# Forty instead of thirty-two tokens by gathered rows, the rest by dense products, in a transformer block with product-key experts

## The chip, the cores and the metric

One Trainium2 chip, one core of it. The metric is device time in microseconds (us) of one execution, lower is better; times given are medians of several runs.

## The reference

One block over 256 tokens of width 2048: latent attention and forgetting attention (8 heads each), a layer norm, and then the part that the change touches, a product-key expert layer ("peer") beside a gated embedding, and a last layer norm.

```python
def peer(h, w_q, keys1, keys2, u_tab, v_tab):          # h: 256 tokens x 2048
    q = (h @ w_q).reshape(b, s, 8, 128)
    s1, s2 = q[..., :64] . keys1, q[..., 64:] . keys2   # 128 scores each, per head
    v1, i1 = top_k(s1, 16); v2, i2 = top_k(s2, 16)
    sc, pos = top_k(all 256 sums of v1 and v2, 16)
    eidx = (i1 * 128 + i2) at pos                       # 16 experts of 16384, for each of 8 heads
    gate = softmax(sc)
    a   = sum_d u_tab[eidx] * h                         # 128 experts a token
    act = gelu(a) * gate
    return sum_k act * v_tab[eidx]                      # rows of 2048
h = layer_norm(ALPHA * h + peer(...) + (p @ w_proj) * sigmoid(h @ w_gate))
```

All of it is float32.

## The kernel before

The 16384 experts are 128 blocks of 128. For most tokens the kernel computes the products with **all** experts (dense) and multiplies by a gate matrix that is zero where an expert wasn't chosen. For the last `TS` = 32 tokens it gathers the rows that were chosen (sparse). `TD` = 256 - `TS` = 224 tokens are dense.

**The dense products.** A float32 weight tile of 128 x 2048 (1024 KB) is loaded by the SP queue into one of three raw buffers (line 74), and each half of it is split into a rounded part `hi` by ScalarE (line 79) and a remainder `lo` by VectorE (line 80), into five buffers of each. `Queue` hands out the halves in the order of use and makes three of them ahead. TensorE multiplies `hi` by the tokens' own hi and lo parts and `lo` by their hi part. For the first 24 u blocks these are three matmuls of `TD` columns for each 128 x 128 piece (`uprod`, line 715). After them come 104 u blocks (`uslots`) and 128 v blocks (`vslots`) in turn, as u, v, u, v, with 27 v blocks alone at the end. Here one matmul takes `hi` with both parts side by side, 2 x `TD` columns (lines 985 and 1015), and one takes `lo` with `TD` columns (lines 986 and 1016): sixteen such pairs for each block. A u block is summed (ScalarE line 974, VectorE line 975), goes through the Gelu (976), is multiplied by its gates (line 964) and split again (968, 969); a v block is added to the accumulator `accT` (998, 999). A u block is made three blocks ahead of its use.

**The gate matrix.** While the first 24 u blocks run, the one-hot products of eight tokens at a time (`gate_onehots`, then `gate_products`, line 769, `TB` = 8) build the gates, ScalarE moves them out of PSUM into `gsb` (line 774), and a group of `TG` = 32 tokens is stored to DRAM in two DMAs by SP (line 777). There are 28 such blocks and seven groups. In the dense products ScalarE's queue loads the gates of four u blocks in one DMA (`gload`, line 955; before the first u block it loads the first). Its destination is in a pool that takes the memory of the pool with the index and gate tiles `xe` and `gg`.

**The sparse tokens.** Each of the 32 tokens has 128 rows of `u` and of `v`. It lies on four partitions (`NQ` = 128 / `TS`), each with 32 of its rows (`NR_`). Lines 905 to 907 issue from POOL (GpSimd) the twelve DMAs that lay out the row numbers, the gates and the token's vector so. Then 64 steps follow, 32 for `u` and 32 for `v`: POOL gathers a row for each partition (line 935, three buffers), and VectorE takes the dot product with the token (line 942) or adds the row times its weight (949). A step stands in some v blocks, by

```python
if not half and ns < 2 * NR_ and (i + 1) * 2 * NR_ >= ns * (NK - NU - PRE - 2):
    sparse(ns)
    ns += 1
```

with `NK` - `NU` - `PRE` - 2 = 99, so that they are spread over the first 98 v blocks, and each step issues the gather three steps ahead. At the end a matmul with the constant `sel` adds the four partitions of each token (`add_y`, line 1048), `finish_columns` transposes the dense results back, and `norm2` does the last layer norm.

The instructions of each engine are issued in the order of the program in this part of the kernel (a manual order); each engine runs its own in order.

Of the kernel before, what the change touches and what calls it, by code (L numbers as in the profile page):

```python
# [16 lines left out]
AF = mybir.ActivationFunctionType  # L17
OP = mybir.AluOpType
AX = mybir.AxisListType

P = 128
# [21 lines left out]
CK = CC["swap"][0]  # L43


TS = 32
TD = T - TS
NQ = P // TS
CB = 8


@with_exitstack
def block_kernel(ctx: ExitStack, tc: tile.TileContext, xT, xn, cst, pos, wz, wkf, wfv, wuq, wuk, wuv, wo, wq, wg, wp,
                 pT, keysT, lnrows, ut, vt, un, vn, out):
    nc = tc.nc
    V, S, G, PE = nc.vector, nc.scalar, nc.gpsimd, nc.tensor
# [8 lines left out]
    def bank(tag, name):  # L65
        return (psA if tag == "A" else psum).tile([P, 512], F32, name=name, tag=tag,
                                                  bufs={"A": 4, "B": 2, "C": 2}[tag])
# [20 lines left out]
    def b8(name, shape, dt=F32):  # L88
        return keep.tile(shape, dt, name=name, tag="b8", bufs=4)
# [4 lines left out]
    def cc(name, p0=0, p1=P):  # L94
        a, b = CC[name]
        return cs[p0:p1, a:b] if b <= CK else cs1[p0:p1, a - CK:b - CK]
# [84 lines left out]
    for g in range(4):  # L181
# [6 lines left out]
        for k0 in range(4 * g, 4 * g + 4, step):  # L188
            c = slice(k0 % 8 * T, (k0 % 8 + step) * T)
            ks = slice(k0, k0 + step)  # L190
            r = xr[g // 2][:, c]
# [167 lines left out]
    for h in range(NH):  # L359
        q_, k_ = head_tile("fq"), head_tile("fk")  # L360
        zs = itertools.chain(zsteps(wz[8 + 2 * h], q_, xhl), zsteps(wz[9 + 2 * h], k_, xhl))
        for i in range(4):
# [7 lines left out]
            h, q_, k_, lambda qb, n, h=h: (fsel[0:F1, h:h + 1].to_broadcast([F1, P]), negF[0:F1, :n]),  # L370
# [50 lines left out]
    for hg in range(2):  # L421
# [4 lines left out]
        for j in range(4):  # L426
            h = hg * 4 + j
            r0 = 64 * (h % 2)
            for _ in attend(
                h, qn[j], kn[j],  # L430
                lambda qb, n, h=h, r0=r0: (qr[h // 2][r0:r0 + 64, qb * P:(qb + 1) * P], kr[r0:r0 + 64, :n]),
# [31 lines left out]
            self.used += 1  # L463
            return self.ready[self.used - 1]

    TG = 32
    TB = 8
    NU, PRE = 24, 3

    NC = NK // CB  # L470
    order = [("u", b) for b in range(NU, NU + PRE)]
# [21 lines left out]
    def tk(name, shape, dt=F32):  # L493
        return pg.tile(shape, dt, name=name, tag="tk", bufs=4)
# [32 lines left out]
    for i in range(2):  # L527
        for c in range(0, D, T):
            nc.sync.dma_start(lnr[i][:, c:c + T], bass.AP(tensor=lnrows.tensor, offset=lnrows.offset + i * D + c,
                                                          ap=[[0, P], [1, T]]))  # L530
# [113 lines left out]
    gst, sel = {}, {}  # L644
# [88 lines left out]

    ND = TD // TG
    gd = dram.tile([ND, P, NK, TG], F32, name="gd")
    iot = pg.tile([P, P, 2], F16, name="iot")
# [21 lines left out]
    def gate_products(b):  # L758
        o = onehot.pop(b)
        g, q = divmod(b, TG // TB)  # L760
        if q == 0:
            gsbs[g] = [b8("gsb", [P, NK // 2, TG]) for _ in range(2)]
        gsb = gsbs[g]
        for q4 in range(TB // 4):
# [7 lines left out]
            for i in range(2):  # L772
                t0 = q * TB + q4 * 4
                S.mul(gsb[i][:, :, t0:t0 + 4], gv[:, i * 64:(i + 1) * 64], 1.0 / GSCALE)
        if q == TG // TB - 1:
            for i in range(2):
# [34 lines left out]

    hd = dram.tile([TS, D], F32, name="hd")
    G.dma_start(hd, acc[P - TS:, 1])

# [39 lines left out]
    n = 0  # L854
# [35 lines left out]
            _, _, f_, a_ = later.pop(0)  # L890
            f_(*a_)

    NR_ = P // NQ
    xg = [tk("xg", [P, P]), tk("xe", [P, P], U32)]
    gi1, gg1 = gst[1][3], gst[1][4]
    V.scalar_tensor_tensor(xg[0], gi1[:, 0], float(NK), gi1[:, 1], op0=OP.mult, op1=OP.add)
    V.tensor_copy(xg[1], xg[0])
    xidx = p2.tile([P, NR_], U32, name="xidx")
    xgate = p2.tile([P, NR_], F32, name="xgate")
    dots = p2.tile([P, NR_], F32, name="dots")  # L900
    hy = b8("hy", [P, D])
    rows = [b8("rows", [P, D]) for _ in range(3)]
    for q in range(NQ):
        qs_, qc = slice(q * TS, (q + 1) * TS), slice(q * NR_, (q + 1) * NR_)
        G.dma_start(xidx[qs_], xg[1][P - TS:, qc])
        G.dma_start(xgate[qs_], gg1[P - TS:, qc])
        G.dma_start(hy[qs_], hd)

    ad = dram.tile([2, P, D], F32, name="ad")
# [15 lines left out]
    def defer(n, f_, *a_):  # L925
        slots[n].append((f_, a_))

    def slot():
        for f_, a_ in slots.pop(0):
            f_(*a_)  # L930
        slots.append([])

    def gather(i):
        if i < 2 * NR_:
            G.indirect_dma_start(out=rows[i % 3], out_offset=None, in_=(un if i < NR_ else vn),  # L935
                                 in_offset=bass.IndirectOffsetOnAxis(ap=xidx[:, i % NR_:i % NR_ + 1], axis=0))

    def sparse(i):

        r, j = rows[i % 3], slice(i % NR_, i % NR_ + 1)  # L940
        if i < NR_:
            V.scalar_tensor_tensor(r, r, 1.0, hy, op0=OP.mult, op1=OP.mult, accum_out=dots[:, j])  # L942
            if i == NR_ - 1:
                S.activation(dots, dots, AF.Gelu)
        elif i == NR_:
            V.tensor_tensor(dots, dots, xgate, op=OP.mult)
            V.tensor_scalar(hy, r, dots[:, j], None, op0=OP.mult)
        else:
            V.scalar_tensor_tensor(hy, r, dots[:, j], hy, op0=OP.mult, op1=OP.add)  # L949
        gather(i + 3)  # L950

    def gload(c):
        if c < NK // GC:
            gbs[c] = p3.tile([P, ND, GC, TG], F32, name="gb", bufs=2)
            nc.scalar.dma_start(gbs[c], bass.AP(tensor=gd.tensor, offset=gd.offset + c * GC * TG,
                                                ap=[[NK * TG, P], [P * NK * TG, ND], [1, GC * TG]]))

    def gated(b):
        c, j = divmod(b, CB)
        if b % GC == 0:  # L960
            gload(b // GC + 1)
        ga = gel.pop(b)
        gv = ga.rearrange("p (g t) -> p g t", t=TG)
        V.tensor_tensor(gv, gv, gbs[b // GC][:, :, b % GC], op=OP.mult)  # L964
        if j == 0:
            acts[c] = p3.tile([P, CB, 2, TD], F32R, name="act", bufs=2)
        at = acts[c][:, j]
        S.copy(at[:, 0], ga)  # L968
        defer(0, lambda: V.tensor_tensor(at[:, 1], ga, at[:, 0].bitcast(F32), op=OP.subtract))  # L969
# [33 lines left out]
    def vslots(i):  # L1003
# [4 lines left out]
        for g in range(2):  # L1008
            hi, lo = queue.get()
            for d in range(2):  # L1010
                o = ps[:, d, :2 * TD].rearrange("p (w t) -> p w t", w=2)
                for j4 in range(4):
                    j = g * 4 + j4
                    col = slice(j4 * 256 + d * P, j4 * 256 + (d + 1) * P)
                    PE.matmul(o, hi[:, col], at[:, j], start=j == 0, stop=False)  # L1015
                    PE.matmul(ps[:, d, :TD], lo[:, col], at[:, j, 0], start=False, stop=j == CB - 1)  # L1016
            slot()
# [27 lines left out]
    def add_y(q):  # L1045
        fin, qs_ = fins[0], slice(q * 512, (q + 1) * 512)
        ps = bank("C", "yps")
        PE.matmul(ps, cc("sel"), hy[:, qs_], start=True, stop=True)
        defer(0, lambda: V.tensor_tensor(fin[:, 1, qs_], fin[:, 1, qs_], ps, op=OP.add))


# [42 lines left out]
    for i in range(3):  # L1094
        gather(i)
    gload(0)
    ns, since = 0, 0
    for n, (w, i) in enumerate(order):
        for half, _ in enumerate(uslots(i) if w == "u" else vslots(i)):
            if n and n < PRE:  # L1100

                for b in range(2):
                    gated(((n - 1) * 2 + half) * 2 + b)
            elif w == "v":
                if half and i + CB < NK:
                    gated(i + CB)
# [4 lines that stand above are left out]
                if i >= NK - NU - PRE + 3 and not half:  # L1111
                    since += 1
                    if since == 1:
                        get_fin()
                    elif 5 <= since < 9:
                        add_y(since - 5)
# [6 lines left out]
def _constants():  # L1123
    c = np.zeros((P, CW), np.float32)
    i = np.arange(P)

    def put(name, a):
        c[:, CC[name][0]:CC[name][1]] = a

    put("ident", np.eye(P))  # L1130
    sw = (i // 64) * 64 + (i % 64 + 32) % 64
    perm = np.zeros((P, P))
    perm[sw, i] = 1.0
    put("swap", perm)
    dup = np.zeros((P, P))
    dup[i % 64, i] = 1.0
    put("dup", dup)
    dsw = np.zeros((P, P))
    dsw[(i % 64 + 32) % 64, i] = 1.0
    put("dupswap", dsw)  # L1140
    put("mean", np.full((P, P), 1.0 / 512))
    put("iota", np.tile(i[None, :], (P, 1)))
    put("sel", (i[None, :] >= P - TS) & (i[:, None] % TS == i[None, :] - (P - TS)))
    fsel = np.zeros((P, NH))
    for r in (0, 32, 64):
        fsel[r + np.arange(NH), np.arange(NH)] = 1.0
    put("fsel", fsel)
    put("mask", np.where(i[None, :] <= i[:, None], 0.0, NEG))
    e = np.arange(0, 64, 2, dtype=np.float32) / np.float32(64)
    freq = (np.float32(1) / np.power(10000.0, e.astype(np.float64)).astype(np.float32)).astype(np.float32)  # L1150
    put("freq", freq[i % 32][:, None])
    put("sign", np.where(i % 64 < 32, -1.0, 1.0)[:, None])
    return c


def _layout(x, p, positions, w_in, b_forget, g_q_norm, w_uq, g_kv_norm, w_ukv, w_out, ln1_g, ln1_b, peer_wq,
# [17 lines left out]
    d["xT"] = A(xt.transpose(1, 0, 2))  # L1174
    d["xn"] = A(x.reshape(2, P, D).transpose(1, 0, 2))
    cst = _constants()

    def put(name, a):
# [59 lines left out]
```

## Time and profile before

| | |
|---|---|
| median of 3 runs | 1937.49 us (1937.35 to 1937.9) |
| the profiled execution | 1937.41 us |
| its span, first to last instruction | 1935.6 us |
| mean granted TensorE clock | 0.983 |
| TensorE, VectorE, ScalarE, GpSimd busy | 96%, 77%, 48%, 15% of the span |
| DMA | 469.86 MB, 243 GB/s over the span |

PE is TensorE's matmuls and PEld its weight loads, DVE is VectorE, ACT is ScalarE, POOL is GpSimd, SP is the engine that issues most loads. A DMA's issue is listed with its queue (SPq, ACTq, or POOL). [...] Matmuls overlap, so the time of one is read from the distance of two starts. Idle time of an engine that doesn't set the pace costs nothing.

### The profile page before, as it was taken

What the parts mean: (1) busy time and instruction counts of PE and PEld (TensorE: products, weight loads), DVE (VectorE), ACT (ScalarE), POOL (GpSimd) and SP (SyncE); (2) the same over time, 40 slices, a digit from 0 to 9 for tenths busy, and PEclk for the clock granted to TensorE, in tenths of its full rate; (3) what the DMA queues carried; (4) which work ended last, traced back from release to release, by engine and by line L of the source; (5) the groups of instructions that cost most, each with busy time, mean ns of one, the idle gap of its engine ahead of it and who ended that gap; (6) DMA issues with size and microseconds to landing.
All of it is one profiled execution on the core that took longest, in us unless ns stands there. A gap on an engine that the chain in (4) does not pass through costs nothing.

```text
span 1935.6 us, 29855 instructions
## 1 busy us (share of the span) xinstructions
PE 1865.9 (96%) x11729; PEld 1708.4 (88%) x11729; DVE 1489.9 (77%) x2307; ACT 927.3 (48%) x1430; POOL 287.2 (15%) x179
## 2 busy tenths in 40 slices
PE   9999999989899997999999999999999999999995
PEld 6888877878699996999999999999999999999895
DVE  6365655689999946887888888788888888877777
ACT  5454544454355534454444454544454554554341
POOL 0343000388300011101110110011010111000001
PEclk9999999999899998999999999999999999999997
DMA  7544434545456788878888888888888888867651
GB/s 288 216 174 148 157 134 144 190 159 178 149 194 237 271 297 306 293 280 293 294 285 298 285 286 294 280 293 290 302 284 286 283 296 289 287 216 278 228 184 66
DMA packets 96925, 469.86 MB, mean 243 GB/s; under 512 B 8304, under 2 KB 39792, under 8 KB 43120
## 3 DMA queue, kind: packets, MB, share of 16 engines
q1 hardware_dynamic: 57168, 380.49, 54.4%
q0 software_dynamic: 9712, 68.46, 10.3%
q10 hardware_dynamic: 29904, 19.01, 3.2%
q8 instruction: 92, 1.51, 0.3%
q14 instruction: 49, 0.40, 0.1%
HBM read 448.75 MB, written 19.14 MB: 242 GB/s over the span
## 4 chain that ended last, share of the span: by engine, by line
PE 87%; DVE 8%; ACT 2%; DMA 1%; issue 1%; ACTq 0%; SPq 0%; POOL 0%; DVEq 0%
PE vps L1015 20%; PE ups L985 18%; PE vps L1016 10%; PE ups L986 9%; PE zps L112 7%; PE ups L715 6%; PE nat L145 4%; PE nat L146 3%; PE nat L144 3%; PE zps L113 3%; DVE lo L80 2%; PE gps L769 1%; ACT hi L79 1%; PE sps L325 1%; DVE cand L637 1%
## 5 line engine op out<-in xcount | busy, mean ns | idle before, releaser
L80 DVE TENSOR_TENSOR lo<-raw,hi 128x1024 fp32r<-128x1024 f32 x618 | 755.0, 1233 | 351.5 <-ACT hi L79 350.7
L79 ACT CAST hi<-raw 128x1024 fp32r<-128x1024 f32 x674 | 703.1, 1049 | 307.4 <-PE ups L985 114.0
L1015 PE MATMUL vps<-act,hi 128*128 128x448 f32 x2048 | 654.3, 376 | 7.2 <-DVE act L969 7.1
L985 PE MATMUL ups<-hl,hi 128*128 128x448 f32 x1664 | 530.8, 374 | 15.5 <-DVE uga L975 15.5
L1016 PE MATMUL vps<-act,lo 128*128 128x224 f32 x2048 | 542.7, 265 | 0.0
L986 PE MATMUL ups<-hl,lo 128*128 128x224 f32 x1664 | 438.8, 264 | 0.0
L1015 PEld LDWEIGHTS vps<-act,hi 128*128 128x128 f32 x2048 | 385.8, 188 | 38.8 <-ACT hi L79 5.3
L1016 PEld LDWEIGHTS vps<-act,lo 128*128 128x128 f32 x2048 | 392.4, 192 | 1.0 <-issue 1.0
L985 PEld LDWEIGHTS ups<-hl,hi 128*128 128x128 f32 x1664 | 312.8, 188 | 41.0 <-issue 15.7
L986 PEld LDWEIGHTS ups<-hl,lo 128*128 128x128 f32 x1664 | 317.8, 191 | 0.0
L968 ACT CAST act<-uga 128x224 fp32r<-128x224 f32 x128 | 48.3, 379 | 308.7 <-DVE uga L964 308.7
L112 PE MATMUL zps<-hl,hi 128*128 128x512 f32 x512 | 185.9, 402 | 5.1 <-DVE hl L555 5.1
L80 POOL TENSOR_TENSOR lo<-raw,hi 128x1024 fp32r<-128x1024 f32 x56 | 136.2, 2441 | 337.1 <-ACT hi L79 309.8
L113 PE MATMUL zps<-hl,lo 128*128 128x256 f32 x512 | 145.3, 284 | 0.5 <-DVE lo L80 0.5
L715 PE MATMUL ups<-hl,hi 128*128 128x224 f32 x768 | 132.5, 277 | 0.0
L112 PEld LDWEIGHTS zps<-hl,hi 128*128 128x128 f32 x512 | 97.1, 190 | 26.2 <-DVE hl L555 6.2
L935 POOL DMA_INDIRECT rows<-in_vn,xidx x32 | 51.9, 1622 | 439.8 <-DVE hy L949 386.4
L715 PEld LDWEIGHTS ups<-hl,hi 128*128 128x128 f32 x768 | 116.5, 192 | 0.1
L935 POOL DMA_INDIRECT rows<-in_un,xidx x32 | 51.2, 1601 | 406.1 <-DVE rows L942 401.4
L974 ACT COPY fold<-ups 128x224 f32<-128x224 f32 x104 | 36.1, 347 | 149.7 <-PE ups L986 149.7
L715 PE MATMUL ups<-hl,lo 128*128 128x224 f32 x384 | 105.4, 274 | 0.0
L113 PEld LDWEIGHTS zps<-hl,lo 128*128 128x128 f32 x512 | 97.8, 191 | 1.0 <-DVE lo L80 1.0
(250 smaller groups left out, 2093.2 us busy)
## 6 DMA issues: line engine op xcount, KB each, us to landing
raw<-in_ut SPq DMA_DIRECT2D x128, 1024.0 KB, 4.8
raw<-in_vt SPq DMA_DIRECT2D x128, 1024.0 KB, 4.9
raw<-in_wz SPq DMA_DIRECT2D x24, 1024.0 KB, 4.8
raw<-in_wo SPq DMA_DIRECT2D x16, 1024.0 KB, 4.8
raw<-in_wg SPq DMA_DIRECT2D x16, 1024.0 KB, 4.8
gd<-gsb SPq DMA_DIRECT2D x14, 1024.0 KB, 8.1
gb<-gd ACTq DMA_DIRECT2D x32, 448.0 KB, 6.4
raw<-in_wq SPq DMA_DIRECT2D x8, 1024.0 KB, 4.8
```

The lines of the kernel that those rows point to most:

```text
L79: S.copy(hi, src)
L80: (lo_eng or V).tensor_tensor(lo, src, hi.bitcast(F32), op=OP.subtract)
L112: PE.matmul(ps, whi, mov, start=first, stop=False)
L113: PE.matmul(ps[:, :T], wlo, mov[:, 0], start=False, stop=last)
L144: PE.matmul(psl[t], st[:, 0, ts], hi[:, c], start=first and j == 0, stop=False)
L145: PE.matmul(psl[t], st[:, 0, ts], lo[:, c], start=False, stop=False)
L715: PE.matmul(ps[:, :TD], w, hhl[:, k, m, :TD], start=k == 0 and w is hi and m == 0, stop=k == KT - 1 and w is lo)
L935: G.indirect_dma_start(out=rows[i % 3], out_offset=None, in_=(un if i < NR_ else vn), in_offset=bass.IndirectOffsetOnAxis(ap=xidx[:, i % N ...
L985: PE.matmul(o, hi[:, s_], hhl[:, k, :, :TD], start=k == 0, stop=False)
L986: PE.matmul(ups[:, :TD], lo[:, s_], hhl[:, k, 0, :TD], start=False, stop=k == KT - 1)
L1015: PE.matmul(o, hi[:, col], at[:, j], start=j == 0, stop=False)
L1016: PE.matmul(ps[:, d, :TD], lo[:, col], at[:, j, 0], start=False, stop=j == CB - 1)
```

## The change

`TS` goes from 32 to 40. Of the sparse tokens each lies on three partitions instead of four (120 of 128 are used, `PS`), with 43, 43 and 42 of its 128 rows; the last partitions' 43rd row is row 0 with a gate of 0, which two new memsets provide. So there are 86 gather steps instead of 64, each of 120 rows, and nine layout DMAs instead of twelve. 216 tokens are dense instead of 224. The gate matrix is stored in nine groups of 24 tokens (`TG`) instead of seven of 32: 27 blocks of eight tokens, and a gate load reads pieces of 4 x 24 numbers.

```diff
-TS = 32
+TS = 40
 TD = T - TS
 NQ = P // TS
+PS = NQ * TS
+NR_ = -(-P // NQ)
...
-    TG = 32
+    TG = 24
...
-    NR_ = P // NQ
...
+    V.memset(xidx, 0)
+    V.memset(xgate, 0.0)
...
     for q in range(NQ):
-        qs_, qc = slice(q * TS, (q + 1) * TS), slice(q * NR_, (q + 1) * NR_)
-        G.dma_start(xidx[qs_], xg[1][P - TS:, qc])
-        G.dma_start(xgate[qs_], gg1[P - TS:, qc])
+        qs_, qc, n = slice(q * TS, (q + 1) * TS), slice(q * NR_, min((q + 1) * NR_, P)), min(NR_, P - q * NR_)
+        G.dma_start(xidx[qs_, :n], xg[1][P - TS:, qc])
+        G.dma_start(xgate[qs_, :n], gg1[P - TS:, qc])
         G.dma_start(hy[qs_], hd)
...
-            G.indirect_dma_start(out=rows[i % 3], out_offset=None, in_=(un if i < NR_ else vn),
-                                 in_offset=bass.IndirectOffsetOnAxis(ap=xidx[:, i % NR_:i % NR_ + 1], axis=0))
+            G.indirect_dma_start(out=rows[i % 3][:PS], out_offset=None, in_=(un if i < NR_ else vn),
+                                 in_offset=bass.IndirectOffsetOnAxis(ap=xidx[:PS, i % NR_:i % NR_ + 1], axis=0))
...
-        r, j = rows[i % 3], slice(i % NR_, i % NR_ + 1)
+        r, j, y = rows[i % 3][:PS], slice(i % NR_, i % NR_ + 1), hy[:PS]
         if i < NR_:
-            V.scalar_tensor_tensor(r, r, 1.0, hy, op0=OP.mult, op1=OP.mult, accum_out=dots[:, j])
+            V.scalar_tensor_tensor(r, r, 1.0, y, op0=OP.mult, op1=OP.mult, accum_out=dots[:PS, j])
...
-    put("sel", (i[None, :] >= P - TS) & (i[:, None] % TS == i[None, :] - (P - TS)))
+    put("sel", (i[None, :] >= P - TS) & (i[:, None] % TS == i[None, :] - (P - TS)) & (i[:, None] < PS))
```

The other lines of the diff only cut the steps' operands to the first `PS` partitions.

## Rows read from the trace of the kernel before

**Rows 1.** The page: busy time, and GB/s in 40 slices of the span.

```profile
PE 1865.9 (96%) x11729; PEld 1708.4 (88%) x11729; DVE 1489.9 (77%) x2307; ACT 927.3 (48%) x1430; POOL 287.2 (15%) x179
...
GB/s 288 216 174 148 157 134 144 190 159 178 149 194 237 271 297 306 293 280 293 294 285 298 285 286 294 280 293 290 302 284 286 283 296 289 287 216 278 228 184 66
```

**Rows 2.** Stages: us, busy us (instructions) of PE, PEld, DVE, ACT, POOL; clock, DMA share, GB/s.

```profile
551.80:711.80 160.00, 157.70 (x1608) 156.24 (x1606) 140.72 (x186) 90.07 (x191) 0.00 (x0) 1.00 0.69 252
711.80:754.60 42.80, 25.19 (x140) 23.43 (x139) 18.37 (x32) 12.85 (x24) 11.51 (x16) 0.80 0.90 309
754.60:1700.00 945.40, 945.40 (x6036) 901.27 (x6036) 773.63 (x945) 467.90 (x663) 97.57 (x60) 1.00 0.82 289
```

**Rows 3.** Groups by line: shapes, count, busy us, mean ns, idle us before.

```profile
L1015 PE MATMUL vps<-act,hi 128*128 128x448 f32 x2048 | 654.3, 376 | 7.2 <-DVE act L969 7.1
L985 PE MATMUL ups<-hl,hi 128*128 128x448 f32 x1664 | 530.8, 374 | 15.5 <-DVE uga L975 15.5
L715 PE MATMUL ups<-hl,hi 128*128 128x224 f32 x768 | 132.5, 277 | 0.0
...
L769 PE MATMUL gps<-onehot 128*128 128x128 f16 x448 | 31.1, 219 | 2.3 <-DVE onehot L754 2.3
```

**Rows 4.** Timeline of PE in the long stage: start us, us, instruction.

```profile
1004.06 0.26 PE L986 MATMUL ups<-hl,lo 128*128 128x224 f32 x1
1004.17 0.37 PE L985 MATMUL ups<-hl,hi 128*128 128x448 f32 x1
```

**Rows 5.** Timeline of the weight loads at the same place.

```profile
1004.07 0.19 PEld L985 LDWEIGHTS ups<-hl,hi 128*128 128x128 f32 x1
```

**Rows 6.** Timeline of PE in an earlier product, 512 and 256 columns.

```profile
119.84 0.39 PE L112 MATMUL zps<-hl,hi 128*128 128x512 f32 x1
120.07 0.28 PE L113 MATMUL zps<-hl,lo 128*128 128x256 f32 x1
120.19 0.39 PE L112 MATMUL zps<-hl,hi 128*128 128x512 f32 x1
...
121.23 0.39 PE L112 MATMUL zps<-hl,hi 128*128 128x512 f32 x1
```

**Rows 7.** Timeline of PE in the first u blocks, two triples apart.

```profile
601.00 0.27 PE L715 MATMUL ups<-hl,lo 128*128 128x224 f32 x1
...
601.67 0.28 PE L715 MATMUL ups<-hl,lo 128*128 128x224 f32 x1
```

**Rows 8.** Waits, 754.6 to 1798 us: waiter, releaser, us in total, times, longest.

```profile
POOL rows L935 <- DVE hy L949: 386.4, 28, 19.0
...
DVE lo L80 <- ACT hi L79: 193.3, 179, 1.6
...
ACT hi L79 <- PE ups L985: 114.0, 97, 1.5
```

**Rows 9.** Groups by line, as rows 3: the sparse steps on VectorE.

```profile
L942 DVE SCALAR_TENSOR_TENSOR rows<-rows,hy 128x2048 f32<-128x2048 f32 x32 | 73.1, 2283 | 0.0
L949 DVE SCALAR_TENSOR_TENSOR hy<-rows,dots,hy 128x2048 f32<-128x2048 f32 x31 | 72.7, 2344 | 0.0
```

**Rows 10.** The page: DMA queue of ACT (packets, MB, share of 16 engines) and weight loads.

```profile
q10 hardware_dynamic: 29904, 19.01, 3.2%
...
raw<-in_ut SPq DMA_DIRECT2D x128, 1024.0 KB, 4.8
```

**Rows 11.** Timelines of POOL, ACT and PE at the hand-over: start us, us, instruction, idle before.

```profile
715.42 0.55 POOL L905 DMA_DIRECT2D xidx<-xe  x1 [195.23 <-DVE xe L897]
...
721.96 0.49 POOL L907 DMA_DIRECT2D hy<-hd  x1 [2.58 <-DMA xidx<-xe]
...
725.05 0.50 POOL L906 DMA_DIRECT2D xgate<-gg  x1 [1.29 <-DMA hy<-hd]
...
729.81 0.38 ACTq L955 DMA_DIRECT2D gb<-gd  x1
...
737.57 0.71 PE L985 MATMUL ups<-hl,hi 128*128 128x448 f32 x1 [15.47 <-DVE uga L975]
```

More of the change, by code (lines that the diff above doesn't have):

```diff
@@ L934, in gather @@
         if i < 2 * NR_:
-            G.indirect_dma_start(out=rows[i % 3], out_offset=None, in_=(un if i < NR_ else vn),
-                                 in_offset=bass.IndirectOffsetOnAxis(ap=xidx[:, i % NR_:i % NR_ + 1], axis=0))
+            G.indirect_dma_start(out=rows[i % 3][:PS], out_offset=None, in_=(un if i < NR_ else vn),
+                                 in_offset=bass.IndirectOffsetOnAxis(ap=xidx[:PS, i % NR_:i % NR_ + 1], axis=0))
     def sparse(i):
-        r, j = rows[i % 3], slice(i % NR_, i % NR_ + 1)
+        r, j, y = rows[i % 3][:PS], slice(i % NR_, i % NR_ + 1), hy[:PS]
         if i < NR_:
-            V.scalar_tensor_tensor(r, r, 1.0, hy, op0=OP.mult, op1=OP.mult, accum_out=dots[:, j])
+            V.scalar_tensor_tensor(r, r, 1.0, y, op0=OP.mult, op1=OP.mult, accum_out=dots[:PS, j])
             if i == NR_ - 1:
-                S.activation(dots, dots, AF.Gelu)
+                S.activation(dots[:PS], dots[:PS], AF.Gelu)
         elif i == NR_:
-            V.tensor_tensor(dots, dots, xgate, op=OP.mult)
-            V.tensor_scalar(hy, r, dots[:, j], None, op0=OP.mult)
+            V.tensor_tensor(dots[:PS], dots[:PS], xgate[:PS], op=OP.mult)
+            V.tensor_scalar(y, r, dots[:PS, j], None, op0=OP.mult)
         else:
-            V.scalar_tensor_tensor(hy, r, dots[:, j], hy, op0=OP.mult, op1=OP.add)
+            V.scalar_tensor_tensor(y, r, dots[:PS, j], y, op0=OP.mult, op1=OP.add)
         gather(i + 3)
@@ L1047, in add_y @@
         ps = bank("C", "yps")
-        PE.matmul(ps, cc("sel"), hy[:, qs_], start=True, stop=True)
+        PE.matmul(ps, cc("sel", 0, PS), hy[:PS, qs_], start=True, stop=True)
         defer(0, lambda: V.tensor_tensor(fin[:, 1, qs_], fin[:, 1, qs_], ps, op=OP.add))
```

## The prediction

> **What bounds the kernel now.** I read the page's busy times first, then the span cut into stages. TensorE is busy 96% of the span [rows 1], far more than any other engine; the stages show that this is no mere average. From 754.6 to 1700 us TensorE is busy in all 945.4 us at full clock, 6036 matmuls without a hole, with VectorE at 773.6 us and the DMA engines at 0.82 [rows 2]. In that stretch (to 1798 us) the view of waits has no line in which TensorE waits; ScalarE's casts wait for TensorE to free a weight buffer (97 times, 114.0 us) and VectorE waits for the casts [rows 8]. So the weight pipeline runs ahead of TensorE and is held back by it: TensorE's pace is the time of this stage. From 551.8 to 711.8 us it is busy 157.7 of 160.0 us, in the first 24 u blocks and the gate products [rows 2]. It waits in only two places: from 711.8 to 754.6 us, where it is busy 25.2 of 42.8 us [rows 2], and in the last stage with its norm.
>
> The profiled execution took 1937.41 us, 1.8 us more than its span, and the median of three is 1937.49: the sum below starts from 1937.4.
>
> **Narrower matmuls, 448 to 432 and 224 to 216 columns.** The hi matmuls of the dense products are 2048 + 1664 = 3712 [rows 3], each followed by one lo matmul of half the width: 3712 pairs. A pair takes 945.4 / 3018 = 313.3 ns [rows 2]. It loses 24 of 672 columns. What a column is worth I bound from both sides. If the time goes with the columns: 313.3 x 24/672 = 11.2 ns, 41.5 us in all. A wider pair of the same kind is in the trace, 512 + 256 columns: four of them from 119.84 to 121.23 us, 347.5 ns each [rows 6]. So 96 columns cost 34.2 ns, 0.356 ns each, and 24 are worth 8.55 ns: 31.7 us. If only the hi matmul shrinks, because the lo one already lasts as long as the weight load beside it, 16 columns are left: 5.7 ns by that slope, 21.1 us. I take 31.7 us, since the row of the other width has the same two loads and overheads in it, and 21.1 to 41.5 as ends.
>
> Whether the load sets the pace: a load starts at 1004.07, 0.01 us after the lo matmul of 1004.06, and the matmul that uses it starts at 1004.17 [rows 4, 5], so the load takes no more than 0.10 us out of an interval of 0.11. That doesn't tell a load that is just hidden from one that just binds. [...]
>
> **The first 24 u blocks.** 768 hi matmuls, half as many lo, 1152 in all, go from 224 to 216 columns [rows 3]. Two triples from 601.00 to 601.67 us are six matmuls, 0.112 us each [rows 7]. There three narrow ones follow each other, so a load has to fit into every one of them, and a gain is less sure than in the pairs: between nothing and 0.112 x 8/224 x 1152 = 4.6 us. I take 2 us. Both ends stay at or below zero, as fewer columns add no instruction.
>
> **One gate block less.** 27 blocks of eight tokens instead of 28. The products took 31.1 us of matmuls for 28 blocks [rows 3], 1.1 us a block, in a stage in which TensorE is full: 1 us less. Their VectorE work lies beside it. Nine groups are stored in 18 DMAs instead of 14, each three quarters as large; SP, which issues them, otherwise only prefetches there: nothing, up to 1 us if a prefetch comes late.
>
> **The hand-over to the dense products.** TensorE stops at about 722 us and goes on at 737.57 [rows 11]. Backwards: it waits for VectorE's sum, which stands behind the first gate rows; ScalarE could issue the load of these only at 729.81 [rows 11], and it is an in-order engine, so its casts stood behind that wait. The load's buffer lies where the pool of the index and gate tiles was, so it waits for the POOL DMAs that read them, of which the last xgate one was issued at 725.05. They are twelve, one every 0.5 us from 715.42, but the ninth waited until 721.96 for the first to land and those after it for others [rows 11]. Now they are nine, and the last xgate one is the eighth. If the queue again lets eight through at once, it goes out at 718.9, 6.1 us earlier; if the budget is one of rows (8 x 32 = 256, so six of 40) the seventh waits until about 722 and the eighth to about 723, 2 us earlier. The larger rows DMAs (320 instead of 256 KB) and the two memsets ahead of the first one can take some of this back: up to 2 us slower. I take 3 us faster, from 6 to minus 2.
>
> **22 more gather steps.** 2 x 43 instead of 2 x 32, still within the first 98 v steps, so 0.88 per u/v round instead of 0.65. On VectorE a step is 2.28 us (dots) or 2.34 us (sums) [rows 9]: 22 x 2.31 = 51 us more in the long stage. I cost them at nothing; the cover is VectorE's idle time. 773.6 + 51 = 825 us, in a stage that shrinks from 945.4 by 3018 x 8.55 ns to 920: 90% busy. What queues behind a step are the lo halves, 2.3 us late at most, and TensorE needs one half in 8 pairs, 2.4 us, with three made ahead. Without the cover each step would cost its 2.3 us. The wait of a step for its rows isn't new: POOL issues a gather as soon as the buffer is free, three steps ahead, and already does so [rows 8].
>
> On the DMA engines a round of 32 pairs (10.0 us) moves two loads of 1024 KB [rows 10], 0.65 of a gather of 1.05 MB and a quarter of the gate rows, 2.89 MB: the 289 GB/s of [rows 2]. Now it is 0.88 of 120 rows, 3.07 MB in 9.75 us: 315 GB/s, a share of 0.82 x 315/289 = 0.89. The gate rows come in pieces of 384 instead of 512 bytes, 9/7 as many. Their queue took 3.2% of the span [rows 10]; at an unchanged time for a piece that is one point more, at twice the time five. [...] Neither price reaches TensorE in my forecast.
>
> **Sum.** 31.7 + 2 + 1 + 3 = 37.7 us less: 1899.7, and I say 1900. The last stages keep their waits.
>
> **Rivals.**
> Only the hi matmul shrinks, the load pins the lo one and the triples: 21.1 to 27.7 (16 columns at 11.2/24 ns each) + 0 + 1 + 3 = 25 to 32 us less, 1905 to 1912. For it: the 0.10 us of load within the 0.11 us interval; against it: from a lo matmul of 256 columns to the next start it is 0.12 us [rows 6], from one of 224 it is 0.11 [rows 4], so width still told there. Chance 0.2.
>
> VectorE or the loads fall short at times: at 90% VectorE and 0.9 of the DMA, some lo halves come late and TensorE pauses, each pause also putting its clock at risk as at 722 us (clock 0.80 in that stage [rows 2]). If a quarter of the 86 steps cost their 2.3 us less a microsecond of lead: 28 us back, 1928; a few: 1910. Against it: today's rounds with a step don't differ from those without. Chance 0.12.
>
> Slower: the DMA engines saturate. A round of 3.07 MB decides at 307 GB/s, where it takes the 10.0 us of before; the highest of the 40 slices is 306 [rows 1]. If the 293 to 297 GB/s of most of those slices were a ceiling, a round would take 10.4 us, 98 rounds 39 us more, less about 9 gained elsewhere: 1968. Against it: 309 GB/s at a share of 0.90 in 711.8 to 754.6 us and 289 at 0.82 [rows 2] both point to 343 to 352 at full share, and the rate of before is what TensorE asked for. Chance 0.04.
>
> The columns are not what a pair pays for (it moves in steps wider than 24 columns, or waits for both loads): only 1 + 3 us, 1933. Against it: the two widths in the trace. Chance 0.04.
>
> **How the numbers follow.** Forecast 0.6, around 1900 (1886 to 1908 by its own bounds: columns proportional and the full six microseconds at one end, a late half now and then at the other); then 0.2, 0.12, 0.04, 0.04. The range has to take in the load-pinned case and the milder half of the late halves: 1885 to 1922; what is left out is the worse part of the starved cases, the two last and a little below. 0.2% (3.9 us) is about what a measurement of this kernel can tell from no change: below 1933.6 is faster. Of the cases only the last sits at that edge, and the saturated one is slower: faster 0.93, same 0.03, slower 0.04.
>
> **What would show it.** Right: in the long stage TensorE is still full, a pair takes about 305 ns (2 x 100 us over the matmuls of 100 us), VectorE about 90%, DMA share about 0.9 at some 315 GB/s, and the waits still name no wait of TensorE there. The hand-over hole is 10 to 14 us instead of 15.7. Pinned loads: pairs at 306 to 308 ns, lo intervals still 0.10, and the triples still 0.112. Starved: TensorE waits for lo halves, and casts that wait for loads instead of for TensorE. What would make the prediction wrong: an access at the new strides (216 columns, 120 rows) that costs more than at the old ones, which no row of before shows.

## The result and the profile after

The changed kernel takes 2031.38 us (median of 4 runs, 2024.84 to 2035.74) against 1937.52 us before: 1.0485 times as long, 95% interval 1.0472 to 1.0499. It is 94 us slower where 37 us faster was forecast. The profiled execution took 2031.05 us, with a span of 2029.3.

In the page of the kernel after, the busy times, the DMA queues (packets, MB, share of 16 engines) and the DMA issues (KB, us to landing) answer to [rows 1, 10]:

```profile
PE 1899.8 (94%) x11713; PEld 1727.7 (85%) x11713; DVE 1529.6 (75%) x2338; ACT 910.1 (45%) x1426; POOL 310.4 (15%) x198
...
q1 hardware_dynamic: 57744, 379.96, 54.4%
q0 software_dynamic: 12832, 85.90, 18.7%
q10 hardware_dynamic: 38096, 18.48, 3.6%
...
raw<-in_ut SPq DMA_DIRECT2D x128, 1024.0 KB, 8.1
raw<-in_vt SPq DMA_DIRECT2D x128, 1024.0 KB, 9.0
```

The gathers run on q0, the weight loads on q1. Before, these queues' lines read so:

```profile
q1 hardware_dynamic: 57168, 380.49, 54.4%
q0 software_dynamic: 9712, 68.46, 10.3%
```

The bytes of the gathers grew by a quarter, their engine time to 1.9 times (10.3% of 1935.6 us to 18.7% of 2029.3 us). The weight loads move nearly the same bytes, and took 1104 us of all sixteen engines instead of 1053. A weight load of 1024 KB lands after 8.1 to 9.0 us instead of 4.8. The stages of the kernel after, with the columns of [rows 2]:

```profile
551.80:710.00 158.20, 155.97 (x1558) 153.42 (x1557) 141.86 (x184) 89.77 (x187) 0.00 (x0) 1.00 0.68 249
710.00:800.00 90.00, 63.55 (x398) 60.64 (x397) 45.06 (x65) 28.30 (x46) 13.38 (x15) 0.85 0.88 246
800.00:1660.00 860.00, 815.36 (x5024) 764.36 (x5023) 674.18 (x816) 376.15 (x550) 101.40 (x69) 0.98 0.97 280
```

and the same stretch of the long stage in the kernel before:

```profile
800.00:1660.00 860.00, 860.00 (x5492) 819.86 (x5491) 701.88 (x858) 424.65 (x601) 89.18 (x55) 1.00 0.82 289
```

TensorE isn't full any more, 5024 matmuls instead of 5492 in 860 us. VectorE and ScalarE are busy less, not more. Only the DMA engines are: a share of 0.97, and yet 280 GB/s instead of 289. Per full share that is 289 GB/s where it was 352. The waits from 760 to 1860 us (waiter, releaser, us in total, times, longest) show how this reaches TensorE; before, the casts waited for TensorE [rows 8]:

```profile
ACT hi L81 <- DMA raw<-in_vt: 194.1, 70, 6.7
PEld vps L1020 <- DVE lo L82: 42.0, 69, 1.1
ACT hi L81 <- DMA raw<-in_ut: 36.9, 30, 3.8
PEld vps L1019 <- ACT hi L81: 32.4, 16, 9.9
...
DVE uga L968 <- DMA gb<-gd: 13.5, 1, 13.5
```

ScalarE's casts wait for loads 231 us, and TensorE's weights wait for the casts and the lo halves behind them. The last line is one hole by itself: at 757 us VectorE stood for 13.5 us before a gate load and ran nothing else. Every profiled execution with gathers of 120 rows has this hole (13.4 to 14.6 us); in the others it is absent or shorter, 7.6 us at most.

### The profile page after: what moved, and what is told of

Same layout as the page of the kernel before. It is cut to its first block, busy times and chain, and to the rows that moved or that the text cites. A ratio compares the mean times of both kernels' runs of the same rounds, so it can differ in the third digit from the quotient of the medians.

```text
span 2029.3 us, 29903 instructions
## 1 busy us (share of the span) xinstructions
PE 1899.8 (94%) x11713; PEld 1727.7 (85%) x11713; DVE 1529.6 (75%) x2338; ACT 910.1 (45%) x1426; POOL 310.4 (15%) x198
## 3 DMA queue, kind: packets, MB, share of 16 engines
q0 software_dynamic: 12832, 85.90, 18.7%
## 4 chain that ended last, share of the span: by engine, by line
PE 45%; DVE 26%; DMA 17%; issue 6%; ACT 5%; ACTq 0%; POOL 0%; DVEq 0%; SPq 0%
DVE lo L82 12%; DMA raw<-in_vt 10%; PE vps L1019 8%; PE zps L114 6%; ACT hi L81 5%; DMA raw<-in_ut 5%; PE ups L989 4%; PE vps L1020 4%; PE ups L717 4%; PE nat L147 3%; PE zps L115 3%; PE nat L146 3%; PE nat L148 3%; PE ups L990 2%; DVE hy L953 2%
## 5 line engine op out<-in xcount | busy, mean ns | idle before, releaser
L81 ACT CAST hi<-raw 128x1024 fp32r<-128x1024 f32 x674 | 692.0, 1046 | 420.4 <-DMA raw<-in_vt 196.5
L1019 PE MATMUL vps<-act,hi 128*128 128x432 f32 x2048 | 671.4, 383 | 39.3 <-ACT hi L81 28.1
L1020 PE MATMUL vps<-act,lo 128*128 128x216 f32 x2048 | 553.8, 270 | 23.2 <-DVE lo L82 21.7
L989 PE MATMUL ups<-hl,hi 128*128 128x432 f32 x1664 | 522.6, 370 | 15.1 <-DVE uga L979 14.9
L990 PE MATMUL ups<-hl,lo 128*128 128x216 f32 x1664 | 441.6, 265 | 3.8 <-DVE lo L82 3.7
L972 ACT CAST act<-uga 128x216 fp32r<-128x216 f32 x128 | 47.4, 373 | 447.9 <-DVE uga L968 447.9
L939 POOL DMA_INDIRECT rows<-in_vn,xidx x43 | 65.3, 1518 | 471.6 <-DVE hy L953 425.1
L939 POOL DMA_INDIRECT rows<-in_un,xidx x43 | 62.5, 1453 | 470.8 <-DVE rows L946 462.8
L717 PE MATMUL ups<-hl,hi 128*128 128x216 f32 x768 | 132.3, 277 | 0.0
L717 PE MATMUL ups<-hl,lo 128*128 128x216 f32 x384 | 105.6, 275 | 0.0
L953 DVE SCALAR_TENSOR_TENSOR hy<-rows,dots,hy 120x2048 f32<-120x2048 f32 x42 | 98.5, 2346 | 0.0
```

The costliest lines, as they stand in the source:

```text
L81: S.copy(hi, src)
L717: PE.matmul(ps[:, :TD], w, hhl[:, k, m, :TD], start=k == 0 and w is hi and m == 0, stop=k == KT - 1 and w is lo)
L939: G.indirect_dma_start(out=rows[i % 3][:PS], out_offset=None, in_=(un if i < NR_ else vn), in_offset=bass.IndirectOffsetOnAxis(ap=xidx[:PS ...
L953: V.scalar_tensor_tensor(y, r, dots[:PS, j], y, op0=OP.mult, op1=OP.add)
L989: PE.matmul(o, hi[:, s_], hhl[:, k, :, :TD], start=k == 0, stop=False)
L990: PE.matmul(ups[:, :TD], lo[:, s_], hhl[:, k, 0, :TD], start=False, stop=k == KT - 1)
```

## The experiments

Three theories fit so far. A: a gather of 120 rows occupies the DMA engines far longer than one of 128. B: it is the gate pieces of 384 bytes. C: it is the number of bytes gathered. A fourth, D, came with the first run, for what is lost with 128 rows: VectorE's own lateness. In the table each ratio is to the kernel before as it was run in the same comparison; its medians lie between 1936.12 and 1937.51 us, so runs of different comparisons are set against each other by their distance from it.

| run | median, us | ratio to before, 95% interval |
|---|---|---|
| e1_gather128 | 1928.22 | 0.9951 (0.9934 to 0.9968) |
| e2_before_120 | 1949.68 | 1.0071 (1.0054 to 1.0087) |
| e3_before_gate256 | 1946.12 | 1.0048 (1.0031 to 1.0065) |
| e4_gate768 | 2026.48 | 1.0461 (1.0419 to 1.0503) |
| e5_short_steps | 1913.98 | 0.9888 (0.9871 to 0.9904) |
| e6_narrow_alone | 1917.78 | 0.9902 (0.9886 to 0.9919) |
| e7_before_112 | 1937.36 | single run |
| e8_before_96 | 1944.61 | single run |
| e9_lo_on_pool | 1919.90 | 0.9917 (0.9897 to 0.9936) |
| e10_dense192 | 1849.64 | single run |
| e11_dense160 | 1809.54 | single run |
| e12_120_short_steps | 2040.60 | 1.0525 (1.0498 to 1.0551) |

**e1_gather128**: the changed kernel, the gathers on all 128 partitions.

```diff
-            G.indirect_dma_start(out=rows[i % 3][:PS], ...
-                                 in_offset=bass.IndirectOffsetOnAxis(ap=xidx[:PS, i % NR_:i % NR_ + 1], axis=0))
+            G.indirect_dma_start(out=rows[i % 3], ...
+                                 in_offset=bass.IndirectOffsetOnAxis(ap=xidx[:, i % NR_:i % NR_ + 1], axis=0))
```

> The changed kernel, but each gather fills all 128 partitions: the last eight fetch row 0 and nothing reads them (eight rows a step more from memory, 90 MB instead of 85). Theory A (a gather of 120 rows lies badly on the DMA engines, one of 128 well): the time falls to 1895 to 1912 us, a pair of matmuls takes 304 to 306 ns, the gather queue's share of the span falls from 18.7% to 13 to 14% although it moves more bytes. Theory B (the gate rows in pieces of 384 bytes clog the engines): stays at 2020 to 2040. Theory C (22 more gathers are too many bytes, however they lie): 2031 to 2050, as there are 6% more of them.

1928.22 us: 103 us less than the changed kernel, by gathering *more*. Its gather queue on the page, and its stage from 800 to 1660 us:

```profile
q0 software_dynamic: 12832, 91.54, 13.5%
```

```profile
800.00:1660.00 860.00, 858.10 (x5507) 822.53 (x5506) 736.27 (x889) 403.60 (x603) 121.28 (x75) 1.00 0.87 313
```

Theories B and C fall: same pieces, more bytes, and the DMA engines move 313 GB/s at a share of 0.87 (360 at full share). Theory A stands. But the time is above the 1895 to 1912 us expected, so something else is lost; the waits of TensorE in this run (760 to 1790 us) name VectorE:

```profile
PEld vps L1020 <- DVE lo L82: 8.7, 29, 0.7
...
PEld vps L1019 <- DVE act L973: 2.1, 5, 0.7
```

**e2_before_120**: the kernel before, with the gathers' row count changed. VectorE also sets the three row buffers to zero once, at the hand-over; e7_before_112 has the same three memsets and takes 1937.36 us.

```diff
+    for r_ in rows:
+        V.memset(r_, 0.0)
...
-            G.indirect_dma_start(out=rows[i % 3], ...
-                                 in_offset=bass.IndirectOffsetOnAxis(ap=xidx[:, i % NR_:i % NR_ + 1], axis=0))
+            G.indirect_dma_start(out=rows[i % 3][:120], ...
+                                 in_offset=bass.IndirectOffsetOnAxis(ap=xidx[:120, i % NR_:i % NR_ + 1], axis=0))
```

> The kernel before with one thing changed: each of its 64 gathers fetches 120 rows instead of 128, so the rows of eight partitions (two rows in a step for each of four... of the sparse tokens' sums) are left out; their buffers are set to zero once. Theory A: the gather queue's share of the span rises from 10.3% to 13 to 15% though its bytes fall by 6%, the DMA share of the long stage from 0.82 to about 0.90, and the time stays at 1937 or rises to 1965 us. Theories B and C: the queue's share falls to about 9.7%, the time is 1933 to 1941.

The gather queue on the page, and the long stage:

```profile
q0 software_dynamic: 9712, 64.27, 14.2%
```

```profile
800.00:1660.00 860.00, 860.00 (x5491) 819.86 (x5491) 703.81 (x860) 424.47 (x603) 91.51 (x56) 1.00 0.91 286
```

Six per cent fewer bytes, 1.4 times the engine time, as theory A says, and the DMA share goes from 0.82 to 0.91. The long stage still runs at TensorE's pace (5491 matmuls); 64 such gathers fit. The 12 us are lost before it, where VectorE waits for a gate load and TensorE behind it (waits from 755 to 780 us), the same hole that the changed kernel has at 757 us:

```profile
DVE uga L966 <- DMA gb<-gd: 14.6, 1, 14.6
PEld vps L1017 <- ACT hi L79: 10.8, 1, 10.8
```

**e7_before_112** and **e8_before_96**: as e2_before_120 with 112 and 96 rows.

> The kernel before with gathers of 112 rows (16 partitions' rows left out). Theory K (a count that isn't shared evenly by all sixteen engines is what costs): 112 is seven rows for each, so the gather queue's share of the span falls below the 10.3% of 128 rows, to about 9%. Theory P (only the full 128 has the good layout of rows on engines): the share stays high, 11 to 14%.

> The kernel before with gathers of 96 rows (32 partitions' rows left out). Theory K: six rows for each engine, the gather queue's share of the span is about 7.7%. Theory P: 9.5 to 12%.

Their gather queues, 112 rows first (span 1935.6 us), then 96 (span 1942.8 us):

```profile
q0 software_dynamic: 8688, 60.07, 11.0%
```

```profile
q0 software_dynamic: 7664, 51.68, 10.1%
```

From bytes, share and span, an engine busy with gathers moves, in GB/s (68.46 MB / (0.103 x 16 x 1935.6 us) for the first):

| rows in a gather | kernel | GB/s per busy engine |
|---|---|---|
| 128 | before | 21.5 |
| 128 | e1_gather128 | 22.0 |
| 120 | after | 14.1 |
| 120 | e2_before_120 | 14.5 |
| 112 | e7_before_112 | 17.6 |
| 96 | e8_before_96 | 16.5 |

The other profiles lie close to these, but for two with VectorE's steps cut short: 128 rows move 21.5 to 22.3 (24.9 in e5_short_steps), 120 rows 14.1 to 14.5 (15.1 in e12_120_short_steps). Every count under 128 that was tried is slower by a sixth or more, and 120 is worst: theory P (only 128 rows lie well), with 96 rows in the range it gave (10.1% of 9.5 to 12) and 112 at its lower end (11.0%). Theory K (a count that sixteen engines can't share evenly) falls: it put 112 rows at 9%.

The trace lists the DMA packets with their sizes and times. A packet of 8 KB in the gather queue, nearly always a row, takes 309 ns (median) in the kernel before, 432 with 112 rows, 492 with 96 and 588 with 120; over 500 ns are 12, 30, 47 and 73 of a hundred. So most rows of a 120-row gather are slow, not a few late ones. The packets on the pages of before and of e2_before_120:

```profile
DMA packets 96925, 469.86 MB, mean 243 GB/s; under 512 B 8304, under 2 KB 39792, under 8 KB 43120
DMA packets 96925, 465.67 MB, mean 239 GB/s; under 512 B 8816, under 2 KB 40304, under 8 KB 43632
```

The 64 gathers of 120 rows have eight small packets more each, 24 instead of 16; with 112 and 96 rows there are 8304 again. In 25 of the 64, nine of these packets of 4 bytes stand back to back at the gather's start. What they have to do with the slower packets no run shows, and 112 and 96 rows, without them, are slower than 128 too (432 and 492 ns against 309). The trace's packets carry no engine, so the trace doesn't show how the rows were shared out. Why 120 is slow stays open; that it is, is measured.

**e3_before_gate256** and **e4_gate768**: the gate pieces.

```diff
-    TG = 32
+    TG = 16
```

```diff
-    GC = 4
+    GC = 8
```

> The kernel before with the gate matrix in fourteen groups of 16 tokens instead of seven of 32: the gate loads read pieces of 256 bytes instead of 512, twice as many. Theory B: pieces under 512 bytes clog the DMA engines, the time rises above 1960 us. Theories A and C: 1932 to 1943, the share of the queue of the gate loads rises from 3.2% to 4 to 6%.

> The changed kernel, but the gates of eight u blocks instead of four come in one load, in pieces of 768 instead of 384 bytes, half as many loads. Theory B: 1950 us or less. Theories A and C: 2020 to 2042, as in the changed kernel.

Pieces of 768 bytes don't help the changed kernel: 2026.48 us, its interval overlaps that of the changed kernel. Pieces of 256 bytes cost the kernel before 8.6 us, between the two expectations. The stretches from 712 to 760 and from 760 to 1700 us of that run, then of the kernel before:

```profile
712.00:760.00 48.00, 26.80 (x140) 24.66 (x139) 18.47 (x32) 13.35 (x25) 11.51 (x16) 0.76 0.88 279
760.00:1700.00 940.00, 940.00 (x6000) 896.11 (x6000) 769.30 (x937) 464.00 (x658) 97.52 (x60) 1.00 0.83 290
```

```profile
712.00:760.00 48.00, 30.39 (x173) 28.36 (x172) 23.21 (x38) 16.82 (x29) 11.51 (x16) 0.82 0.91 314
760.00:1700.00 940.00, 940.00 (x6002) 896.13 (x6001) 768.79 (x940) 463.93 (x657) 97.57 (x60) 1.00 0.82 288
```

The long stage is the same, with the share of the DMA at 0.83 instead of 0.82. What was lost in the profiled execution (5.7 us by its span) lies at the hand-over, 33 matmuls behind at 760 us, in the stage in which TensorE waits for the first gates in the kernel before, too. The engines aren't clogged in the long stage: theory B falls here as well.

**e5_short_steps**: as e1_gather128, with VectorE working on 64 of 2048 columns in each of the 86 steps.

```diff
-            V.scalar_tensor_tensor(r, r, 1.0, y, op0=OP.mult, op1=OP.mult, accum_out=dots[:PS, j])
+            V.scalar_tensor_tensor(r[:, :64], r[:, :64], 1.0, y[:, :64], op0=OP.mult, op1=OP.mult, accum_out=dots[:PS, j])
...
-            V.scalar_tensor_tensor(y, r, dots[:PS, j], y, op0=OP.mult, op1=OP.add)
+            V.scalar_tensor_tensor(y[:, :64], r[:, :64], dots[:PS, j], y[:, :64], op0=OP.mult, op1=OP.add)
```

> The changed kernel with gathers of 128 rows (as the run named e1_gather128), but in each of the 86 steps VectorE works on 64 of the 2048 columns only, so most of the dot products and sums are left out; the gathers, their order and their waits stay. Theory D (what the 128-row version still loses beside its narrower matmuls is lateness of VectorE): 1911 to 1918 us instead of 1928, and TensorE's waits for lo halves, 29 in that run, vanish. Theory E (it is lost to the DMA engines, at a share of 0.87 to 0.89): 1925 to 1931.

The long stage:

```profile
800.00:1660.00 860.00, 860.00 (x5592) 834.76 (x5591) 608.29 (x901) 436.42 (x611) 70.30 (x75) 1.00 0.87 317
```

1913.98 us, 22.2 under the kernel before where e1_gather128 is 9.3 under: TensorE is full again at the same DMA share of 0.87, and its waits for lo halves are gone. Theory D. The run shortens all 86 steps, the 64 old ones too.

**e6_narrow_alone**: the kernel before with 216 dense tokens and gate groups of 24, its gathers untouched.

```diff
-TD = T - TS
+TD = T - TS - 8
...
-    TG = 32
+    TG = 24
```

> The kernel before with its 64 gathers of 128 rows for 32 tokens, but only 216 tokens in the dense products and nine gate groups of 24: the expert part of eight tokens is left out. This is the narrower matmul and the gate matrix of the change alone. By the pair times read in the runs so far (307.3 ns in u blocks, 308.7 in v blocks, against 313.7 and 312.9) 3712 pairs are worth 18 to 20 us and the first 24 u blocks nothing, with one gate block less: 1916 to 1920 us. By the prediction's step (8.55 ns a pair, 2 us in the first u blocks): 1902 to 1905. If gate pieces of 384 bytes cost time by themselves, as those of 256 seem to: 1922 to 1930.

The long stage:

```profile
800.00:1660.00 860.00, 860.00 (x5580) 836.11 (x5579) 707.36 (x871) 430.09 (x612) 91.76 (x57) 1.00 0.83 293
```

1917.78 us, 18.4 less than before in the same comparison. TensorE is full; a pair takes 860/2790 = 308.2 ns instead of 860/2746 = 313.2. So the narrower matmuls are worth 5.0 x 3712 = 18.6 us, all of the gain, and pieces of 384 bytes cost nothing that can be seen in the median. The profiled execution was the longest of the five, 1927.9 us (the others 1915.65 to 1920.2); it has a wait of 7.6 us for gates before 750 us, ahead of the stretch shown.

**e10_dense192** and **e11_dense160**: the width again, 192 and 160 dense tokens (`TD = T - TS - 32`, and `- 64`).

> The kernel before with 192 instead of 224 tokens in the dense products (the expert part of 32 tokens is left out), so matmuls of 384 and 192 columns; the gathers are as before. Theory F (a column is worth what it was worth between 224 and 216, about 0.23 ns, the rest being fixed by the weight loads): a pair takes 288 to 294 ns, the first u blocks stay at 0.1115 us a matmul. [...]

> The kernel before with 160 tokens in the dense products (the expert part of 64 tokens is left out), matmuls of 320 and 160 columns. If two weight loads set a floor, each at the 0.1115 us that the first u blocks show for three narrow matmuls, a pair can't be under 223 ns. [...] In the first u blocks 0.1115 us again if the load sets the pace there. DMA engines or VectorE may set the pace of the whole, so the pair times are what counts, not the time.

Pairs in the long stage, timeline of PE (start us, us, instruction), 192 tokens:

```profile
899.92 0.36 PE L1015 MATMUL vps<-act,hi 128*128 128x384 f32 x1
...
902.23 0.36 PE L1015 MATMUL vps<-act,hi 128*128 128x384 f32 x1
```

and 160 tokens, with the first u blocks of the same run below:

```profile
901.77 0.35 PE L985 MATMUL ups<-hl,hi 128*128 128x320 f32 x1
901.96 0.24 PE L986 MATMUL ups<-hl,lo 128*128 128x160 f32 x1
902.03 0.35 PE L985 MATMUL ups<-hl,hi 128*128 128x320 f32 x1
902.22 0.24 PE L986 MATMUL ups<-hl,lo 128*128 128x160 f32 x1
902.29 0.34 PE L985 MATMUL ups<-hl,hi 128*128 128x320 f32 x1
```

```profile
600.73 0.27 PE L715 MATMUL ups<-hl,lo 128*128 128x160 f32 x1
...
602.41 0.28 PE L715 MATMUL ups<-hl,lo 128*128 128x160 f32 x1
```

Eight pairs in 2.31 us are 289 ns for 576 columns, and 480 columns take 260 ns: from 313.2 at 672 that is 0.25 and 0.28 ns a column. Theory F fits the first (288 to 294); for the second its 0.23 ns a column gives 269 ns, an estimate from 313.2 ns and 192 columns less, and 260 is 9 ns under that. From a lo matmul to the next hi one it is 0.07 us, where it is 0.11 at 224 columns [rows 4]. In the first u blocks five triples take 1.68 us, 0.112 us a matmul, the same as at 224 columns [rows 7].

**e9_lo_on_pool**: as e1_gather128, with one of eight lo halves made by GpSimd.

```diff
-                  + [((ut if w == "u" else vt)[i], (V, V)) for w, i in order])
+                  + [((ut if w == "u" else vt)[i], (V, G if n_ % 4 == 3 else V)) for n_, (w, i) in enumerate(order)])
```

> The changed kernel with gathers of 128 rows (as e1_gather128), and one of every eight lo halves of the dense products is made by GpSimd instead of VectorE (0.57 us less for VectorE in a round of 32 pairs; one on GpSimd takes 2.44 us, as read from the lo rows on POOL). Theory D (VectorE's lateness costs the 128-row version some 14 us): 1917 to 1925 us, a good half of the loss comes back. Against it, GpSimd is late or slows VectorE: 1927 to 1940.

1919.90 us, 16.2 under the kernel before where e1_gather128 is 9.3 under: more than half of the loss comes back, as theory D expects, though the intervals of the two runs just touch. It doesn't come back by the relief that was expected. VectorE is busy 744 of 860 us in the long stage, where it was 736. The lo halves on VectorE from 760 to 1790 us, in e1_gather128 and then here:

```profile
L82 DVE TENSOR_TENSOR lo<-raw,hi 128x1024 fp32r<-128x1024 f32 x413 | 494.4, 1220 | 149.4 <-ACT hi L81 149.4
L82 DVE TENSOR_TENSOR lo<-raw,hi 128x1024 fp32r<-128x1024 f32 x364 | 491.5, 1375 | 140.4 <-ACT hi L81 140.3
```

With GpSimd at work on the same kind of operation, one on VectorE takes 1375 ns instead of 1220, which uses up what the 49 fewer had saved. What did change is who is waited for: TensorE's weight loads no longer wait for VectorE's lo halves, but 12 times, 5.8 us in all, for GpSimd's. This is the whole computation, 0.8% faster than the kernel before and 5.5% faster than the changed one.

**e12_120_short_steps**: e5_short_steps with the changed kernel's 120 rows.

> The changed kernel with its gathers of 120 rows, but in each step VectorE works on 64 of 2048 columns, as in e5_short_steps (most of the dot products and sums are left out). If the DMA engines alone set the pace of the changed kernel: 2005 to 2031 us, with a DMA share of 0.95 or more in the long stage and casts that wait for loads. If it takes both, the slow gathers and the 51 us more on VectorE: 1930 to 1970, and the share well under 0.95.

The long stage, and the wait of the casts for loads (760 to 1860 us):

```profile
800.00:1660.00 860.00, 805.04 (x4964) 747.30 (x4962) 529.66 (x803) 371.55 (x544) 77.11 (x67) 0.99 0.97 277
```

```profile
ACT hi L81 <- DMA raw<-in_vt: 308.4, 74, 7.1
```

2040.60 us, no faster than the changed kernel though VectorE is relieved (529.66 instead of 674.18 us busy). So the DMA engines, at 0.97, set the pace of the changed kernel even with most of VectorE's work in the steps gone. That it is 9 us slower still wasn't expected and isn't explained.

In e2_before_120, e7_before_112 and e8_before_96 the rows of the last partitions, in e6_narrow_alone, e10_dense192 and e11_dense160 the expert part of 8, 32 and 64 tokens, and in e5_short_steps and e12_120_short_steps most of the sparse tokens' products are left out.

## Why the prediction was wrong

From the kernel before to the changed one in three steps, each run by its distance from the kernel before in its own comparison: the narrower matmuls with their gate matrix, -18.4 us (e6_narrow_alone); the 22 further steps with gathers of 128 rows, from there to -9.3 (e1_gather128), so +9.1; 120 rows instead of 128, from there to +93.9, so +103.2. Such steps make up the whole by construction; that each has its cause is shown by the runs above.

**The gather on the DMA engines: the step that failed.** It put "0.88 of 120 rows, 3.07 MB in 9.75 us" at the bytes' share of a 128-row gather: 0.89. The bytes were right, the engine time for them was not: 14.1 instead of 21.5 GB/s per busy engine. At the rate of before, the 85.90 MB would have cost 3995 engine-us, 250 us of all sixteen; they cost 6072, 380 us. To these extra 130 us come the 51 us more that the weight loads took beside them. The forecast share of 0.89 left about 100 us idle in a long stage of 920, an estimate, so it couldn't take them in. The break-even that the prediction gave, 307 GB/s, holds: the changed kernel gets 280, at which a round of 3.07 MB takes 11.0 us, and 98 rounds some 95 us more than before. So the slower rival had the place (the DMA engines saturate, casts wait for loads) and the sign, but its price was taken from what the engines carried on demand, the 293 to 297 GB/s of most slices, and dismissed with the capacity at 128 rows. The row count of a gather was named in the last sentence as something that no row of before shows, and still carried no chance: an unpriced change of layout on DMA engines that were 82% busy should have been a rival. Why a gather of 120 rows is slow stays open. Some of the 103 us may have another cause: in the profiled execution POOL's first layout DMA, ahead of every gather, goes out at 720.35 us, in e1_gather128 at 713.71, and in e4_gate768, with the same 120 rows, at 716.40. Nothing here explains that.

**The columns.** The mechanism was right, the size wrong: 5.0 ns a pair, not 8.55, 18.6 us instead of 31.7. The slope had been taken from the pair of 512 and 256 columns in another product [rows 6]; within the dense products a column is worth 0.21 ns from 672 to 648, and 0.25 and 0.28 ns over the whole way to 576 and 480. The lower end, 21.1, was still too high. The three signs of the rival with pinned loads came true at 216 columns: 308 ns a pair, 0.10 us from a lo matmul to the next hi one, 0.112 us in the triples. The narrower runs show that its mechanism is still not what happens. Over the long stage the time from a lo matmul to the next hi one is 102, 99, 88 and 75 ns (medians) at 224, 216, 192 and 160 columns, about 0.4 ns a column; from a hi matmul to its lo one it is 211, 208, 199 and 185 ns, about 0.2 ns a column. So the lo matmul does shrink, and a column of it is worth about twice a column of the wide one. Why, these runs don't settle.

**The first u blocks.** 2 us were expected, none came. In the kernel after, four triples take 1.34 us, 0.112 us a matmul:

```profile
600.32 0.27 PE L717 MATMUL ups<-hl,lo 128*128 128x216 f32 x1
...
601.66 0.27 PE L717 MATMUL ups<-hl,lo 128*128 128x216 f32 x1
```

It is 0.112 us at 224, 216 and 160 columns, so something other than the width sets the pace there. That it is the weight load, no run here shows. Whatever it is did not pin the lo matmul of a pair, as the 75 ns above show.

**The gate matrix.** The queue of the gate loads in e6_narrow_alone (pieces of 384 bytes) and in e3_before_gate256 (256), against 3.2% before (512) [rows 10]:

```profile
q10 hardware_dynamic: 38096, 18.48, 3.4%
q10 hardware_dynamic: 58576, 19.01, 4.1%
```

Per busy engine that is 19.2 GB/s with 512 bytes, 17.6 with 384 and 14.9 with 256: smaller pieces are slower, but nowhere near the doubled time for a piece that the prediction weighed. The step at nothing, and the one gate block less, were right within what e6_narrow_alone can tell.

**The hand-over.** The nine POOL DMAs did go as the better branch said, eight without a wait. The timelines of POOL and ACT in the kernel after:

```profile
720.35 0.56 POOL L909 DMA_DIRECT2D xidx<-xe  x1 [194.11 <-DVE xgate L904]
...
723.99 0.51 POOL L910 DMA_DIRECT2D xgate<-gg  x1
...
734.17 0.38 ACTq L959 DMA_DIRECT2D gb<-gd  x1
```

and the DMA issues of the kernel after (KB, us to landing) have for the last of them

```profile
xgate<-gg POOLq DMA_DIRECT2D x1, 6.6 KB, 10.1
```

The last xgate goes out 3.6 us after the first DMA instead of 9.6 [rows 11], but lands after 10.1 us, so ScalarE's gate load starts 13.8 us after the first instead of 14.4. What the queue no longer delays, the landing does: 0.6 us instead of 3, and nothing in e1_gather128, where that load starts 14.5 us after the first DMA.

**The 22 steps at nothing.** With 128 rows VectorE is busy 736 of 860 us, 86%, less than the 90% of the prediction, and still TensorE is late now and then: 9.1 us for 22 steps, 0.41 us each of 2.31. The cover held for four fifths. The starved rival had this mechanism, at 10 to 28 us; e5_short_steps shows that VectorE's steps are its cause. e9_lo_on_pool fits with late lo halves, but did not make VectorE less busy.

## What to carry to other kernels

Before a change touches the shape of a DMA, and above all its partition count, look whether any transfer of that shape is in the trace; if there is none, its price per byte is unknown, and here, on DMA engines that were 82% busy, it decided the sign. Padding a gather of 120 rows to 128 moved 7% more bytes in the gathers and made the kernel 5% faster. And a matmul's width is worth what it is worth in the same loop: here narrow ones in a row gained nothing from fewer columns (0.112 us each at 224 and at 160), and where they alternate with wide ones only part of the time went with the columns (313.2 ns a pair at 672, 260 at 480).

## What the runs showed of the hardware

An indirect gather of 8 KB rows moved 21.5 to 24.9 GB/s per busy DMA engine with 128 rows, 17.6 with 112, 16.5 with 96 and 14.1 to 15.1 with 120; the packet of a row took 309, 432, 492 and 588 ns (medians; before, e7_before_112, e8_before_96, e2_before_120). Three float32 matmuls in a row with a weight load each took 0.112 us apiece at 160, 216 and 224 columns alike. A pair of a wide and a narrow one took 313.2, 308.2, 289 and 260 ns at 672, 648, 576 and 480 columns. A subtraction of 128x1024 on VectorE took 1220 ns, and 1375 (means) where GpSimd made one of every eight lo halves.
